# Attention with sinks with its value products turned round, gate steps and low parts of weights moved, and part of an expert search brought forward

## The chip, the core and the metric

One core of a Trainium2 chip runs the whole program. The metric is the device time of one execution in microseconds (us). The engines are PE (TensorE: matmuls and transposes), DVE (VectorE), ACT (ScalarE), POOL (GpSimd) and the DMA queues, which SP issues. Each engine works through its own list of instructions in order; semaphores hold an instruction until what it reads is written and what it overwrites is free.

## The reference

512 tokens of 1024 channels go through four stages in float32: (a) a gated delta-rule mixer; (b) attention in a window of 128 keys with a learned sink per head; (m) a mixer of an mLSTM and a forgetting attention; (p) a product-key retrieval over 16384 single-neuron experts. The parts that the change touches:

```python
# stage b: 32 query heads of 64, 4 key/value heads, blocks of 128 queries and 256 keys
m = max(max(logits), sink); p = exp(logits - m)
probs = p / (sum(p) + exp(sink - m))
o = probs @ v                       # per head
out = (o * silu(z)) @ w_out
# stage p: 8 heads, two half queries each, 128 sub-keys per half
val, idx = top_k(scores, 16)        # per token, head and half
cand = val[:, :, 0, :, None] + val[:, :, 1, None, :]      # 256 candidates
top_s, pos = top_k(cand, 16); gate = softmax(top_s)
```

## The kernel before, in words

A projection of float32 accuracy is three matmuls (`mm3`, lines 315 to 317): every weight panel of 128 x 1024 and the normed tokens are split into a rounded high part (`whi`, `hThi`) and the rest (`wlo`, `hTlo`). The high part of a panel is written by ACT (line 233, or 230 with a gain), the low part by DVE or, where `lo_on_pool` is true, by POOL (line 235). A `Feed` loads panels through SP into `wraw` and splits them ahead of use; its list `srcs` sets the order of the loads.

Most of the program is handed to a scheduler of the framework, which fixes each engine's list when the program is built; the order in which the code issues steps is its input. `weave` interleaves lists of steps in proportion to their lengths.

*Stage b* (`stage_b`, `block_b`). For each of four groups `g` of 8 heads there are queries (`queries`, 96 matmuls of 512 columns), gates (`gates`, 96 of them, tokens in the rows of the result), the attention itself and the output projection (`outputs`). The attention of a group has 8 units `u`: 4 blocks `n` of 128 queries times 2 halves `b` of 4 heads. `logits` (line 920) writes scores to PSUM, DVE adds the bias and takes the limit (line 923), ACT takes the exponential (line 929); `values` transposes the probabilities to `PT` (line 940, copies at 942); `products` (line 951) takes each head's `PT` tile of 128 x 128 as the weights and streams 64 columns of `V`; `finish` divides by the sum on DVE (line 958) and multiplies with the gate on POOL (line 960); `turn` transposes the result (line 966) and splits it into `yh` and `yl`. The attention of group g is woven with gates(g), outputs(g - 1) and queries(g + 1).

*Stage m*. The feed has 36 panels, whose low parts are POOL's. Projections of keys and queries are 36 steps; the mLSTM's gates are 11 small steps (`gates_m`), of which one is issued at step 4 and the others are woven with the next projection.

*Stage p*. `route1` norms and transposes the four token tiles, then for 16 half heads `hp` projects, takes scores (line 1593) and the 16 best of 128 for each tile with `top16` on DVE (lines 1565 to 1569). `route2` has for each token tile t eight steps `head(h)`, each the sum of two lists of 16 (`cand`, line 1613) and a `top16` over 256, and then gates, rows and a finish; `build_g` (DVE lines 1677 and 1682, POOL 1680 and 1684, PE 1690) spreads the chosen experts into a table in DRAM. Between them runs `First.work`, the first projection of blocks of experts (384 columns). The eight heads of tile 1 are issued after `route1`, woven with six such blocks. After `build_g` a list written by hand streams all experts (the last third of the time).

Of the kernel before, what the change touches and what calls it, by code (L numbers as in the profile page):

```python
# [7 lines left out]
F32 = mybir.dt.float32  # L8
# [10 lines left out]
P = 128  # L19
# [718 lines left out]
def stage_b(k):  # L738
    tc, nc, a = k.tc, k.nc, k.a
    with pool(tc, name="sb1", bufs=1) as s1:  # L740
# [12 lines left out]
        srcs, at = kv + wb(0), {("q", 0): 4}  # L753
        for g in range(4):
            for n, l in (("z", wb(4 + g)), ("o", wo(g - 1) if g else []), ("q", wb(g + 1) if g < 3 else [])):
                at[n, g - (n == "o") + (n == "q")] = len(srcs)
                srcs = srcs + l
# [4 lines left out]
        def keys(s2, acc):  # L762
            def use(t, p):
                kv = s2.tile([P, 512], F32, tag="sz", name="kv", bufs=6)
# [43 lines left out]
        def gates(g, s2):  # L808
            d = gs[g]

            def use(t, p):

                z = s2.tile([P, 512], F32, tag="sz", name="sz", bufs=6)
                nc.scalar.activation(z, p, AF.Tanh, scale=0.5)
                nc.vector.scalar_tensor_tensor(z, z, 1.0, p, op0=ALU.add, op1=ALU.mult)
                d["z"].append(z)

            return tiles_steps(k, feed, at["z", g], tiles, hh, hl, use)
# [16 lines left out]
        with pool(tc, name="sb2", bufs=1) as s2:  # L835
            with pool(tc, name="pgb", bufs=2, space=PSUM) as k.pg:
# [21 lines left out]
                for _, f in qs:  # L858
                    f()
            with pool(tc, name="pb", bufs=2, space=PSUM) as k.pb:  # L860
                pt = lambda: k.pb.tile([P, 512], F32, tag="pt", name="pt")
                left = []
                for g in range(4):
                    L, V_, O_, F, T_ = block_b(k, s1, s2, g, gs[g], kT, V, sinkrow)

                    attend = [lambda L=L: L(0)] + left
                    for u in range(8):
# [3 lines left out]
                        if u % 2 == 0 and u:  # L871
                            attend.append(lambda T_=T_, u=u: T_(u // 2 - 1))
                            if u == 4:
                                cut = len(attend) + 1
# [3 lines left out]
                    left = [lambda T_=T_: T_(NT - 1)]  # L878
                    fill = gates(g, s2)
                    if g:  # L880
                        fill += outputs(g - 1, (0, 1), False) + outputs(g - 1, (2, 3), False)
                    if g < 3:
                        qs = queries(g + 1, s2, pt)
                        left.append(qs[-1][1])
# [9 lines left out]
def block_b(k, s1, s2, g, d, kT, V, sinkrow):  # L894
# [37 lines left out]
    def values(u):  # L932
# [3 lines left out]
        for q in range(nst):  # L936
            pt = k.pb.tile([P, 512], F32, tag="pt", name="pt")
            for i in range(4):
                h, st = divmod(4 * q + i, nst)
                nc.tensor.transpose(pt[:, i * P : (i + 1) * P], lg[:, h, st * P : (st + 1) * P], k.ident)  # L940
            eng = nc.vector.tensor_copy if q else nc.scalar.copy
            eng(PT[:, 4 * q : 4 * q + 4, :], v4(pt))

    def products(u):
# [4 lines left out]
        for h in range(4):  # L949
            for st in range(nst):  # L950
                nc.tensor.matmul(d["po"][:, (4 * b + h) * 64 : (4 * b + h + 1) * 64], PT[:, h * nst + st, :],  # L951
                                 V[:, s0 // P + st, g * 64 : (g + 1) * 64], start=(st == 0), stop=(st == nst - 1))

    def finish(n):
        den = d["den", n]
        nc.vector.reciprocal(den, den)
        obs[n] = o = s2.tile([P, 512], F32, tag="ob", name="ob", bufs=2)
        nc.vector.tensor_tensor(out=o.rearrange("p (h c) -> p h c", h=8), in0=d["po"].rearrange("p (h c) -> p h c", h=8),
                                in1=den.rearrange("p (h o) -> p h o", o=1).to_broadcast([P, 8, 64]), op=ALU.mult)
        nc.gpsimd.tensor_tensor(out=o, in0=o, in1=d["z"][n], op=ALU.mult)  # L960

    def turn(n):
        o, ts = obs.pop(n), slice(n * P, (n + 1) * P)
        pt = v4(k.pb.tile([P, 512], F32, tag="pt", name="pt"))
        for i in range(4):
# [768 lines left out]
```

## Time and profile before

| what | value |
|---|---|
| median of 3 runs | 2784.94 us (2783.59 to 2785.3) |
| the profiled execution | 2783.23 us, its span 2781.5 us |
| PE, PEld, DVE busy | 96%, 80%, 71% of the span |
| ACT, POOL busy | 41%, 29% of the span |
| granted clock of TensorE | 0.986 of full speed in the mean |
| DMA | 440.92 MB, 159 GB/s in the mean |

The profile is of one execution. Matmuls are pipelined, so that the duration of one (about 0.40 us for 512 columns) is longer than the distance to the start of the next (about 0.23 us); costs of PE are read from start to start. A float32 matmul or transpose that is not split has records of its own: a matmul of line 951 has two (448 records for 224 matmuls). Groups of the trace name tiles as out<-in. Stages in the span: a to 612 us, b to 1082, m to 1447, p from there, with `route1` to 1574, `route2` and `build_g` to 1900.

### The profile page before, as it was taken

Reading aid. Unit: us, or ns where it says so; the run is one execution under the profiler, and the core shown is the slowest. Engines: PE = TensorE matmul, PEld = TensorE weight load, DVE = VectorE, ACT = ScalarE, POOL = GpSimd, SP = SyncE. Lnnn points to the kernel's source line nnn. Section 1 sums busy time; section 2 is a strip of 40 time slices with the busy share of each in tenths; the row PEclk is TensorE's granted clock in tenths of the full one; section 3 lists DMA queues with packets and bytes.
Section 4 is the critical chain, followed back from the end, with each engine's and each line's share of the span. In section 5 each row is a group of like instructions: output and inputs, shape, how many; then the busy total and the mean of one; then the engine's idle time right before and its main releaser. Section 6 shows DMA issues by size and latency. Waiting matters only on the chain.

```text
span 2781.5 us, 39306 instructions
## 1 busy us (share of the span) xinstructions
PE 2678.8 (96%) x14291; PEld 2222.2 (80%) x14291; DVE 1968.2 (71%) x4299; ACT 1127.4 (41%) x2304; POOL 810.0 (29%) x593
## 2 busy tenths in 40 slices
PE   7999999989999999999989898999999999999999
PEld 5777777767777777677668788999888888888887
DVE  6666666666666654646656999986777777878887
ACT  5444444434444343334422256554333333333333
POOL 0100000000000013232213158774444444444441
PEclk9999999999999999999999999999999999999999
DMA  4111111122222222211122244558999999898996
GB/s 153 53 54 61 54 61 54 46 69 76 65 72 76 68 69 68 61 61 31 32 105 70 87 159 172 184 203 284 325 329 327 321 320 329 312 324 317 329 322 234
DMA packets 170462, 440.92 MB, mean 159 GB/s; under 512 B 13932, under 2 KB 79756, under 8 KB 168604
## 3 DMA queue, kind: packets, MB, share of 16 engines
q1 hardware_dynamic: 133404, 304.17, 33.1%
q0 software_dynamic: 36864, 134.23, 12.7%
q8 instruction: 113, 1.85, 0.3%
q14 instruction: 81, 0.66, 0.1%
HBM read 401.60 MB, written 36.75 MB: 158 GB/s over the span
## 4 chain that ended last, share of the span: by engine, by line
PE 72%; DVE 14%; ACT 5%; issue 5%; POOL 2%; DMA 2%; SPq 0%; ACTq 0%; DVEq 0%; POOLq 0%
PE pj L315 12%; PE pj L316 12%; PE pj L317 12%; PE acc L316 4%; PE acc L317 4%; PE acc L315 4%; PE pG L1690 2%; PE po L951 2%; ACT whio L233 2%; DVE x L1558 1%; DVE wloo L235 1%; PE pl L920 1%; PE po L316 1%; PE po L315 1%; PE po L317 1%
## 5 line engine op out<-in xcount | busy, mean ns | idle before, releaser
L315 PE MATMUL pj<-hThi,whi 128*128 128x384 f32 (+2 forms) x1664 | 604.1, 363 | 2.7 <-ACT hg L1436 2.1
L317 PE MATMUL pj<-hThi,wlo 128*128 128x384 f32 (+2 forms) x1664 | 594.5, 357 | 11.9 <-DVE wlo L235 11.9
L316 PE MATMUL pj<-hTlo,whi 128*128 128x384 f32 (+2 forms) x1664 | 598.6, 360 | 0.0
L317 PEld LDWEIGHTS pj<-hThi,wlo 128*128 128x128 f32 x1664 | 317.8, 191 | 33.8 <-DVE wlo L235 12.5
L315 PEld LDWEIGHTS pj<-hThi,whi 128*128 128x128 f32 x1664 | 317.9, 191 | 32.6 <-ACT hg L1436 2.7
L316 PEld LDWEIGHTS pj<-hTlo,whi 128*128 128x128 f32 x1664 | 318.2, 191 | 25.0 <-issue 1.3
L316 PE MATMUL acc<-wloo,Wh 128*128 128x512 f32 x768 | 302.9, 394 | 4.0 <-DVE wloo L235 2.4
L315 PE MATMUL acc<-whio,Wh 128*128 128x512 f32 x768 | 300.8, 392 | 0.8 <-ACT whio L233 0.8
L317 PE MATMUL acc<-whio,Wl 128*128 128x512 f32 x768 | 300.3, 391 | 0.0
L1549 POOL DMA_INDIRECT raw<-in_v_dram,ids x128 | 192.1, 1501 | 236.1 <-DVE wloo L235 122.8
L1549 POOL DMA_INDIRECT raw<-in_u_dram,ids x128 | 185.8, 1452 | 241.4 <-DVE wloo L235 114.9
L212 ACT CAST Wh<-W 128x384 fp32r<-128x384 f32 x128 | 65.7, 513 | 372.5 <-DVE W L1496 335.7
L235 DVE TENSOR_TENSOR wlo<-raw,whi 128x1024 fp32r<-128x1024 f32 x128 | 161.5, 1262 | 71.9 <-ACT whi L233 71.8
L233 ACT CAST whi<-raw 128x1024 fp32r<-128x1024 f32 x144 | 150.3, 1043 | 123.3 <-issue 90.1
L235 DVE TENSOR_TENSOR wloo<-raw,whio 128x1024 fp32r<-128x1024 f32 x128 | 156.9, 1226 | 52.2 <-ACT whio L233 52.2
L316 PEld LDWEIGHTS acc<-wloo,Wh 128*128 128x128 f32 x768 | 144.2, 188 | 44.4 <-DVE wloo L235 16.8
L317 PEld LDWEIGHTS acc<-whio,Wl 128*128 128x128 f32 x768 | 144.2, 188 | 30.4
L315 PEld LDWEIGHTS acc<-whio,Wh 128*128 128x128 f32 x768 | 144.1, 188 | 29.5 <-ACT whio L233 1.6
L1558 DVE SCALAR_TENSOR_TENSOR x<-raw,act,x 128x1024 f32<-128x1024 f32 x128 | 163.8, 1280 | 1.0
L1553 DVE SCALAR_TENSOR_TENSOR raw<-raw,xt 128x1024 f32<-128x1024 f32 x128 | 154.0, 1219 | 0.0
L233 ACT CAST whi<-wraw 128x1024 fp32r<-128x1024 f32 x100 | 104.6, 1048 | 113.7 <-PE pj L316 70.0
L1436 ACT ACTIVATE hg<-pj 128x384 f32<-128x384 f32 x128 | 62.6, 489 | 190.1 <-PE pj L317 190.1
(423 smaller groups left out, 5417.8 us busy)
## 6 DMA issues: line engine op xcount, KB each, us to landing
raw<-in_uT_dram SPq DMA_DIRECT2D x128, 512.0 KB
raw<-in_v_dram SPq DMA_DIRECT2D x128, 512.0 KB
wraw<-in_wa_dram SPq DMA_DIRECT2D x48, 512.0 KB
G<-stage SPq DMA_DIRECT2D x12, 2048.0 KB
Gt<-G SPq DMA_DIRECT2D x32, 768.0 KB
wraw<-in_wb_dram SPq DMA_DIRECT2D x32, 512.0 KB
wraw<-in_wmt_dram SPq DMA_DIRECT2D x20, 512.0 KB
H<-hg SPq DMA_DIRECT2D x48, 192.0 KB
```

Source lines behind the costliest of these rows:

```text
L212: self.nc.scalar.copy(hi, src)
L233: nc.scalar.copy(hi, raw)
L235: eng.tensor_tensor(out=lo, in0=raw, in1=hi.bitcast(F32), op=ALU.subtract)
L315: nc.tensor.matmul(out, wh, mh, start=first, stop=False)
L316: nc.tensor.matmul(out, wh, ml, start=False, stop=False)
L317: nc.tensor.matmul(out, wl, mh, start=False, stop=last)
L951: nc.tensor.matmul(d["po"][:, (4 * b + h) * 64 : (4 * b + h + 1) * 64], PT[:, h * nst + st, :], V[:, s0 // P + st, g * 64 : (g + 1) * 64], ...
L1436: nc.scalar.activation(hg, p[:, 0:ND], AF.Gelu)
L1549: nc.gpsimd.indirect_dma_start(out=g, out_offset=None, in_=src, in_offset=bass.IndirectOffsetOnAxis(ap=ids[:, j : j + 1], axis=0))
L1553: nc.vector.scalar_tensor_tensor(g, g, 1.0, xt0, op0=ALU.mult, op1=ALU.mult, accum_out=act[:, j : j + 1])
L1558: nc.vector.scalar_tensor_tensor(k.x[:, 0, :], g, act[:, j : j + 1], k.x[:, 0, :], op0=ALU.mult, op1=ALU.add)
L1690: nc.tensor.matmul(p[:, n * P : (n + 1) * P], o1[:, n, :], o0[:, n, :], start=True, stop=True)
```

## The change

In stage b the probabilities are streamed and `V` is the weight: a matmul takes 64 columns of `V` and streams two heads (256 columns), and the two heads of a pair (`j`) write to the two halves of the array's columns. The result has channels in its rows, so it needs no transposing; the gates are projected with channels in rows too, and the reciprocal sums are spread by ACT over 64 columns per head, transposed by PE and multiplied into the gate (`sums`). The gates of group g are computed one group earlier, those of group 0 ahead of the attention. In stage m the low parts go from POOL to DVE and the gate steps are issued at every fourth step from step 5. In stage p the norm of a tile is issued one tile ahead, the low parts of the first two panels go to DVE, and head(h) of tile 1 is issued after half head 2h + 1 of `route1`. The rest of the diff only passes pools and tiles along.

```diff
-        srcs, at = kv + wb(0), {("q", 0): 4}
+        srcs, at = kv + wb(0) + wb(4), {("q", 0): 4, ("z", 0): 8}
         for g in range(4):
-            for n, l in (("z", wb(4 + g)), ("o", wo(g - 1) if g else []), ("q", wb(g + 1) if g < 3 else [])):
+            for n, h, l in (("o", g - 1, wo(g - 1) if g else []), ("q", g + 1, wb(g + 1) if g < 3 else []), ("z", g + 1, wb(5 + g) if g < 3 else [])):
...
+            def step(j, c):
+                if j == c == 0:
+                    d["z"] = s2.tile([P, 4, T], F32, tag="sz", name="sz", bufs=2)
+                if c == 0:
+                    d["p"] = k.acc()
+                p, (wh, wl) = d["p"], feed.get(at["z", g] + c, 1)[0]
+                for i in range(2):
+                    kt, ws = 2 * c + i, slice(512 * i + P * j, 512 * i + P * j + P)
+                    mm3(nc, p, wh[:, ws], wl[:, ws], hh[:, kt, 0:T], hl[:, kt, 0:T], kt == 0, kt == KD - 1)
...
-                for _, f in qs:
+                for _, f in qs + gates(0, s2):
...
-                        if u % 2 == 0 and u:
-                            attend.append(lambda T_=T_, u=u: T_(u // 2 - 1))
+                        if u % 2:
+                            attend.append(lambda S=S, u=u: S(u // 2))
...
-                    fill = gates(g, s2)
+                    fill = []
                     if g:
                         fill += outputs(g - 1, (0, 1), False) + outputs(g - 1, (2, 3), False)
...
-                        weave(attend, fill + qs[:-1])
+                        weave(attend, fill + qs[:-1] + gates(g + 1, s2))
                         continue
                     o = outputs(3, range(4), True)
-                    weave(attend[:cut], fill)
-                    weave(attend[cut:] + left, o[:4])
+                    weave(attend, fill + o[:4])
...
+        if b:
+            den = d["den", n]
+            nc.vector.reciprocal(den, den)
+            obs[n] = ob = s2.tile([P, 4, P], F32, tag="ob", name="ob", bufs=2)
+            nc.scalar.copy(ob.rearrange("p i (j c) -> p (i j) c", j=2), den.rearrange("p (h o) -> p h o", o=1).to_broadcast([P, 8, 64]))
+
+    def sums(n):
...
+            nc.tensor.transpose(pt[:, i * P : (i + 1) * P], ob[:, i, :], k.ident)
+        nc.vector.tensor_tensor(out=z, in0=v4(pt), in1=z, op=ALU.mult)
...
-        for h in range(4):
-            for st in range(nst):
-                nc.tensor.matmul(d["po"][:, (4 * b + h) * 64 : (4 * b + h + 1) * 64], PT[:, h * nst + st, :],
-                                 V[:, s0 // P + st, g * 64 : (g + 1) * 64], start=(st == 0), stop=(st == nst - 1))
+        for st in range(nst):
+            for j in range(2):
+                nc.tensor.matmul(d["po"][64 * j : 64 * j + 64, 2 * b * P : 2 * (b + 1) * P], V[:, s0 // P + st, g * 64 : (g + 1) * 64],
+                                 PT[:, 4 * st + 2 * j : 4 * st + 2 * j + 2, :].rearrange("p i c -> p (i c)"), start=(st == 0), stop=(st == nst - 1))
...
     def finish(n):
...
-        nc.gpsimd.tensor_tensor(out=o, in0=o, in1=d["z"][n], op=ALU.mult)
...
+        nc.vector.tensor_tensor(out=o, in0=v4(d["po"]), in1=d["z"][:, :, ts], op=ALU.mult)
+        k.split(d["yh"][:, :, ts], d["yl"][:, :, ts], o)
...
-                + [(a["wmt"][4 + c], None) for c in range(4)] + [(a["wmo"][4 * c + 2 * h + j], None) for h in range(2) for c in range(2) for j in range(2)], 6)
+                + [(a["wmt"][4 + c], None) for c in range(4)] + [(a["wmo"][4 * c + 2 * h + j], None) for h in range(2) for c in range(2) for j in range(2)], 6, lo_on_pool=False)
...
-                        if n == 4:
+                        if n % 4 == 1 and n > 4:
                             gates.pop(0)()
...
-                route1(k, raw, s0, s2, hh, hl, xt0, val, idx)
+                route1(k, raw, s0, s2, hh, hl, xt0, val, idx, route[1][0][0:8])
...
-                weave(route[1][0], early(n))
+                weave(route[1][0][8:], early(n))
...
     for t in range(NT):
-        xn = k.normed(s0, t, k.rms(s0, t), g)
-        if t == 0:
-            nc.gpsimd.tensor_copy(xt0, xn)
+        nx = norm(t + 1) if t + 1 < NT else None
         k.turn(xn, hh, hl, t * P)
+        xn = nx
...
-        pan = k.halves(r, lo_on_pool=True, bufs=2)
+        pan = k.halves(r, lo_on_pool=hp > 1, bufs=2)
...
+        if hp % 2:
+            heads[hp // 2]()
```

What moves is seen best in the engines' lists. PE in stage b, around one unit's value products (`po` is their result, `pj` that of a projection). Before:

```order
L315 MATMUL pj<-whi,yh 128x512
L316 MATMUL pj<-wlo,yh 128x512
L317 MATMUL pj<-whi,yl 128x512
L951 MATMUL po<-V,PT 128x64 x8
L315 MATMUL pj<-whi,yh 128x512
```

After the change:

```order
L962 MATMUL pt<-cst,ob 128x128 x4
L315 MATMUL pj<-whi,hThi 128x512
L316 MATMUL pj<-wlo,hThi 128x512
L317 MATMUL pj<-whi,hTlo 128x512
L315 MATMUL pj<-whi,hThi 128x512
L316 MATMUL pj<-wlo,hThi 128x512
L317 MATMUL pj<-whi,hTlo 128x512
L973 MATMUL po<-PT,V 64x256 x4
L315 MATMUL pj<-whi,hThi 128x512
```

Eight matmuls of 64 columns have become four of 256 columns on half of the array's columns. Of 24 units with two key tiles 20 have their four in one piece, three have two and two, one has one and three; the 8 units with one key tile have two.

DVE in stage m, where the forgetting attention begins (`fqn` is a normed query tile, `colR` and `colC` gate columns, `dB` a tile of decay). Before:

```order
L310 TENSOR_TENSOR fqn<-pq,rr 128x512
L1219 COPY colR<-pt 16x96
L1220 COPY colC<-pt 16x8
L1219 COPY colR<-pt 128x96
L1220 COPY colC<-pt 128x8
...
L1347 TENSOR_SCALAR dB<-ncB,colC 128x144 x2
L1347 TENSOR_SCALAR dB<-ncB,colC 128x272
L1360 ISA dB,fmm<-pl,dB 128x144
```

After the change:

```order
L310 TENSOR_TENSOR fqn<-pq,rr 128x512
L235 TENSOR_TENSOR wlo<-wraw,whi 128x1024
L1233 COPY colR<-pt 128x96
L1234 COPY colC<-pt 128x8
...
L235 TENSOR_TENSOR wlo<-wraw,whi 128x1024 x2
L1361 TENSOR_SCALAR dB<-ncB,colC 128x144
L235 TENSOR_TENSOR wlo<-wraw,whi 128x1024
L1361 TENSOR_SCALAR dB<-ncB,colC 128x144
L1361 TENSOR_SCALAR dB<-ncB,colC 128x272
L235 TENSOR_TENSOR wlo<-wraw,whi 128x1024
```

Low parts that stood in POOL's list now stand between DVE's steps of the attention.

DVE at the end of `route1` (`psc` are scores, `cand` and `top` belong to a head). Before, the list goes on after the last scores with eight heads:

```order
L235 TENSOR_TENSOR wlo<-raw,whi 128x1024
L1568 MAX val<-scr 128x8
L1569 MAX_INDEX idx<-val,scr 128x8
L1613 TENSOR_TENSOR cand<-val 128x256 x2
L1565 MAX top<-cand 128x8 x2
L1566 MAX_INDEX pos<-top,cand 128x8
```

After the change only the eighth head is left there, and rows follow:

```order
L1636 TENSOR_TENSOR cand<-val 128x256
L1586 MAX val<-scr 128x8
L1583 MAX top<-cand 128x8
L1587 MAX_INDEX idx<-val,scr 128x8
...
L1661 CAST xf<-idx 128x128
L1586 MAX top<-scr_13943 128x8
L235 TENSOR_TENSOR wlo<-raw,whi 128x1024
L1587 MAX_INDEX pos<-top,scr_13943 128x8
L1644 TENSOR_TENSOR pe<-top 128x128
```

Seven heads have moved up between the `top16` of `route1`, and the third block's low part now comes behind one head, not behind seven.

## Rows read from the trace of the kernel before

**Rows 1.** Busy time by stretch: window, PE, PEld, DVE, ACT, POOL, clock, DMA.

```profile
690.00:1060.00 370.00, 363.77 (x2015) 289.51 (x2015) 226.98 (x664) 162.81 (x439) 25.40 (x18) 1.00 0.22 68
...
1082.00:1200.00 118.00, 110.14 (x514) 84.57 (x513) 57.35 (x147) 39.15 (x55) 31.52 (x16) 0.97 0.21 65
1200.00:1447.00 247.00, 240.17 (x1386) 175.61 (x1385) 141.57 (x431) 93.99 (x235) 60.60 (x51) 0.97 0.14 42
1447.00:1470.00 23.00, 13.91 (x61) 11.02 (x60) 11.22 (x21) 7.79 (x13) 6.48 (x3) 0.78 0.58 226
1470.00:1574.00 104.00, 104.00 (x517) 85.84 (x516) 85.06 (x516) 25.83 (x33) 31.46 (x14) 1.00 0.27 82
1574.00:1840.00 266.00, 235.31 (x1482) 230.00 (x1481) 260.03 (x548) 147.04 (x313) 172.44 (x114) 0.95 0.47 165
```

**Rows 2.** Waits of PE, 685 to 1082 us: total, times, longest.

```profile
PE pt L797 <- DVE qn L310: 3.7, 6, 0.9
```

**Rows 3.** Waits of PE, 1080 to 1440 us.

```profile
PE pt L1034 <- DVE rr L188: 5.4, 1, 5.4
PE ptz L1108 <- DVE so L1059: 3.4, 1, 3.4
PE pc L278 <- ACT ncB L1331: 1.5, 1, 1.5
```

**Rows 4.** Waits of PE, 1440 to 1900 us.

```profile
PE pj L317 <- DVE wlo L235: 11.9, 2, 8.9
...
PE pt L264 <- DVE xn L254: 7.8, 1, 7.8
```

**Rows 5.** Timeline of PE in stage b: start, time, instructions merged.

```profile
708.14 1.89 PE L951 MATMUL po<-V,PT 128*128 128x64 f32 x16
709.84 0.48 PE L315 MATMUL pj<-whi,hThi 128*128 128x512 f32 x1
...
711.41 1.14 PE L920 MATMUL pl<-kT,qT 64*128 64x256 f32 x8
712.48 0.50 PE L315 MATMUL pj<-whi,hThi 128*128 128x512 f32 x1
```

**Rows 6.** Timeline of PE in stage m, value products of the forgetting attention.

```profile
1254.09 0.28 PE L316 MATMUL pj<-hTlo,whi 128*128 128x264 f32 x1
1254.20 0.28 PE L317 MATMUL pj<-hThi,wlo 128*128 128x264 f32 x1
1254.42 1.23 PE L1378 MATMUL fo<-fPT,FV 16*64 16x128 f32 x14
1255.58 0.91 PE L1288 MATMUL pS<-mqk,mqk 128*128 128x384 f32 x2
```

**Rows 7.** Groups by line and shape, 690 to 1060 us: DVE's low parts, ACT's copies.

```profile
L235 DVE TENSOR_TENSOR wlo<-wraw,whi 128x1024 fp32r<-128x1024 f32 x16 | 20.5, 1286 | 5.6 <-ACT whi L233 5.6
L942 ACT COPY PT<-pt 128x512 f32<-128x512 f32 x32 | 18.5, 579 | 20.3 <-PE pt L940 20.2
```

**Rows 8.** Groups by line and shape, POOL, 1075 to 1440 us.

```profile
L235 POOL TENSOR_TENSOR wlo<-wraw,whi 128x1024 fp32r<-128x1024 f32 x33 | 80.9, 2461 | 131.5 <-ACT whi L233 129.5 <-DVE dB L1347 2.0
```

**Rows 9.** Timeline of DVE in stage m, during two low parts of POOL.

```profile
1137.52 2.21 DVE L198 SCALAR_TENSOR_TENSOR rr<-rt,rr 128x8 f32<-128x8 f32 x1
1139.65 0.16 DVE L186 TENSOR_SCALAR rt<-rv 128x8 uint32<-128x8 uint32 x1
1139.72 2.84 DVE L213 TENSOR_TENSOR grow<-gu,grow 4x528 fp32r<-4x528 f32 x1
```

**Rows 10.** Busy time by stretch, just after that wait (columns as in rows 1).

```profile
1143.30:1149.20 5.90, 5.89 (x16) 4.75 (x17) 5.16 (x14) 2.86 (x4) 1.33 (x1) 0.50 0.24 83
```

**Rows 11.** Waits of DVE, 1470 to 1574 us.

```profile
DVE val L1565 <- PE psc L1593: 26.3, 16, 8.9
```

**Rows 12.** Timeline of DVE after route1: two heads' first instructions.

```profile
1584.25 0.41 DVE L1613 TENSOR_TENSOR cand<-val 128x256 f32<-128x256 f32 x1
...
1586.42 0.41 DVE L1613 TENSOR_TENSOR cand<-val 128x256 f32<-128x256 f32 x1
```

More of the change, by code (lines that the diff above doesn't have):

```diff
@@ L809, in gates @@
             d = gs[g]
[L811 to L818, printed above, removed]
+            def step(j, c):
[7 more added lines that the diff above has]
+                    mm3(nc, p, wh[:, ws], wl[:, ws], hh[:, kt, 0:T], hl[:, kt, 0:T], kt == 0, kt == KD - 1)
+                if j == 3:
+                    feed.done = at["z", g] + c + 1
+                if c == 3:
+                    z = d["z"][:, j, :]
+                    nc.scalar.activation(z, p, AF.Tanh, scale=0.5)
+                    nc.vector.scalar_tensor_tensor(z, z, 1.0, p, op0=ALU.add, op1=ALU.mult)
+                feed.step()
+            return [(1.3, lambda j=j, c=c: step(j, c)) for j in range(4) for c in range(4)]
         def outputs(g, js, last):
@@ L948, in products @@
             d["po"] = k.pb.tile([P, 512], F32, tag="pv", name="po", bufs=1)
-        for h in range(4):
-            for st in range(nst):
-                nc.tensor.matmul(d["po"][:, (4 * b + h) * 64 : (4 * b + h + 1) * 64], PT[:, h * nst + st, :],
-                                 V[:, s0 // P + st, g * 64 : (g + 1) * 64], start=(st == 0), stop=(st == nst - 1))
+        for st in range(nst):
+            for j in range(2):
+                nc.tensor.matmul(d["po"][64 * j : 64 * j + 64, 2 * b * P : 2 * (b + 1) * P], V[:, s0 // P + st, g * 64 : (g + 1) * 64],
+                                 PT[:, 4 * st + 2 * j : 4 * st + 2 * j + 2, :].rearrange("p i c -> p (i c)"), start=(st == 0), stop=(st == nst - 1))
     def finish(n):
[L955 to L959, printed above, removed]
-        nc.gpsimd.tensor_tensor(out=o, in0=o, in1=d["z"][n], op=ALU.mult)
[L962 to L965, printed above, removed]
-            nc.tensor.transpose(pt[:, i, :], o[:, i * P : (i + 1) * P], k.ident)
-        k.split(d["yh"][:, :, ts], d["yl"][:, :, ts], pt)
-    return logits, values, products, finish, turn
+        ts = slice(n * P, (n + 1) * P)
+        o = s2.tile([P, 4, P], F32, tag="ob", name="ob", bufs=2)
+        nc.vector.tensor_tensor(out=o, in0=v4(d["po"]), in1=d["z"][:, :, ts], op=ALU.mult)
+        k.split(d["yh"][:, :, ts], d["yl"][:, :, ts], o)
+    return logits, values, products, sums, finish
 def stage_m(k):
@@ L1458, in stage_p @@
         early = lambda n: [f.all for f in take(firsts, n)]
-        with pool(tc, name="pg", bufs=4, space=PSUM) as k.pg, pool(tc, name="spT", bufs=1) as sT:
+        with pool(tc, name="pg", bufs=4, space=PSUM) as k.pg, pool(tc, name="spT", bufs=1) as sT, ExitStack() as es:
             val = sT.tile([P, NT, 16, 16], F32, name="val")
             idx = sT.tile([P, NT, 16, 16], U32, name="idx")
+            sh = es.enter_context(pool(tc, name="sph", bufs=2))
+            where = {}
+            route = [route2(k, sh, where, t, val, idx, ids, gate0) for t in range(NT)]
             with pool(tc, name="spr", bufs=1) as s0, pool(tc, name="spr2", bufs=2) as s2:
-                route1(k, raw, s0, s2, hh, hl, xt0, val, idx)
+                route1(k, raw, s0, s2, hh, hl, xt0, val, idx, route[1][0][0:8])
             with pool(tc, name="sps", bufs=1) as s0, pool(tc, name="sps2", bufs=2) as s2:
@@ L1466, in stage_p @@
                 nc.vector.tensor_copy(iota16, k.c["iota"][:, 0:16])
-                route = [route2(k, s0, s2, t, val, idx, ids, gate0, iota16) for t in range(NT)]
+                where.update(s0=s0, s2=s2, iota16=iota16)
                 n = SPILL // 8
-                weave(route[1][0], early(n))
+                weave(route[1][0][8:], early(n))
                 for t in range(1, NT):
@@ L1569, in top16, with route1 @@
     nc.vector.max_index(out=idx[:, 8:16], in_max=val[:, 8:16], in_values=scr)
-def route1(k, raw, s0, s2, hh, hl, xt0, val, idx):
+def route1(k, raw, s0, s2, hh, hl, xt0, val, idx, heads):
     tc, nc, a = k.tc, k.nc, k.a
@@ L1654, in finish @@
             nc.tensor.transpose(pt[:, i * P : (i + 1) * P], s, k.ident)
-        res["selT"] = s2.tile([P, 3, P], F32, tag="selT", name="selT")
+        res["selT"] = where["s2"].tile([P, 3, P], F32, tag="selT", name="selT")
         nc.scalar.copy(res["selT"], pt[:, 0 : 3 * P].rearrange("p (i c) -> p i c", i=3))
```

43 lines of the change are left out of this document (23 added, 20 removed).

## The prediction

> **What bounds the kernel now.** I read the busy times by stretch first [rows 1]. The reader is to see three kinds of stretch. In stage b, 690 to 1060 us, PE is busy 364 of 370 us at full clock, DVE 227, ACT 163: PE sets the time, and what is taken from PE there shortens the program. In stage m, 1082 to 1447, PE is busy 350 of 365, DVE only 199, and the clock is 0.97: PE again, with a few stops. In stage p the two parts differ: in `route1`, 1470 to 1574, PE is busy all the time and DVE 85 of 104; from 1574 to 1840 DVE is busy 260 of 266 and PE 235, so there DVE sets the time. At 1447 to 1470 neither is full: a chain. Then I read what PE waits for in each. In b the largest is 3.7 us in six pieces [rows 2], so next to nothing; in m three waits of 5.4, 3.4 and 1.5 us [rows 3]; in p 11.9 us for low parts of panels on DVE, of which one wait is 8.9 us, and 7.8 us for a normed tile [rows 4].
>
> **The change, part by part.** The sum is made against the profiled execution, 2783.2 us; the median of the runs, 2784.9, lies 1.7 above it.
>
> *1. Value products.* A unit with two key tiles is 16 records of 64 columns from 708.14 to the next start at 709.84, 1.70 us [rows 5]; the 8 units with one key tile have half of that, 0.85. Before: 24 x 1.70 + 8 x 0.85 = 47.6 us, all of it on PE. After, such a unit is 8 records of 256 columns on two halves of the array's columns. Two rows are near. The scores are 8 records of 256 columns too, on two halves of the array's rows, and take 711.41 to 712.48, 1.07 us [rows 5]. The value products of the forgetting attention have just the new arrangement, halves of the columns: 16 records of 128 columns (two are missing in the row), which is the same number of columns, take 1254.42 to 1255.58, 1.16 us, and the matmul ahead of them needs 0.22 us to their start where its neighbour needs 0.11 [rows 6]. I take the second, as it is the same arrangement: 1.16 + 0.10 = 1.26 us for eight records. For a piece of four I take no gain, 0.85. By the order of the changed list there are 20 pieces of eight, 14 of four, and one unit in pieces of two and six (1.7 at most): 25.2 + 11.9 + 1.7 = 38.8 us. Gain 47.6 - 38.8, **-9 us**. Bounds: at 1.07 for eight and 0.64 for four, without anything at the ends, 21.4 + 9.0 + 1.3 = 31.7, a gain of 16; if the halves don't overlap, eight records of 256 columns cost the five steps of 1.07 made eight, 1.7, and the entry of 0.1 for 36 pieces makes it 4 slower.
>
> The Trainium skill (TensorEngine Tiling (Array Packing), Key Properties) says that changing the tiling mode drains the array. It speaks against many short pieces, and the 0.22 us of rows 6 agrees; without it the gain would be the 16, with it the 9.
>
> *2. The rest of stage b.* The 64 transposes of the result are replaced by 64 of the spread sums, equal. The gates have the same 96 matmuls per group; those of group 0 now stand without attention beside them, and the attention of group 3 has 22 us less beside it. I cost that at nothing: PE is the full engine wherever they stand. ACT gets 16 copies of 0.58 us [rows 7], DVE 16 multiplications of 512 values, about 0.64 by half of the 1.29 for 1024 [rows 7], and POOL loses 16. This is hidden under PE; without that cover it would be 20 us. SP issues the same 52 loads with queries ahead of gates; PE waits for no panel in rows 2.
>
> *3. Low parts in stage m.* 36 panels leave POOL, where one takes 2.46 us [rows 8], and cost DVE 36 x 1.29 = 46 us [rows 7]. DVE has 365 - 199 = 166 us free there [rows 1], so it does not fill. What leaves is a stop: while POOL writes low parts, a DVE instruction on 8 values takes 2.21 us and one on 528 values 2.84, where a third on 8 values between them takes 0.16 [rows 9]. These two stand in the chain to the 5.4 us wait of PE [rows 3], and behind it PE runs 5.9 us at a clock of 0.50 [rows 10], that is 1.2 GHz after an idle stretch, which loses another 2.9. The gate steps, which fill DVE there too, are spread out. Of these 8.3 us I take 7 as gone, since low parts of 1.29 us now stand in the same chain. The wait of 3.4 us [rows 3] has a POOL low part beside it as well, but a DVE low part now stands just ahead of the awaited instruction: I take 2. Of the 1.5 us, which ACT ends, 1. Together **-10 us**. Bounds: -15 if all these go with their slow clock; +5 if each of the 36 passes on a tenth of itself and nothing goes.
>
> *4. Start of stage p.* PE waits 7.8 us for the last normed tile [rows 4]. The code issues it earlier, but it needs the last sum of stage m in any case, and the list of DVE has it where it was. Two low parts, 2 x 1.29, enter that chain and a stop like that of rows 9 leaves it: **-1 us**, bounds 0 and -5.
>
> *5. Heads.* Two heads start 1584.25 and 1586.42, 2.17 us apart [rows 12]; eight are 17.4 us of DVE. They leave the stretch where DVE is full [rows 1] and enter `route1`, where DVE waits 26.3 us in 16 pieces for scores, 8.9 of them at the start, so 17.4 in use [rows 11]. That just fits: at 6.5 us per half head, two of them leave 2 x 1.2 us for one head of 2.17. The last head needs the last scores and stays behind: 17.4 - 2.2 = 15.2 us gained on DVE. PE's 8.9 us wait for a low part behind these heads [rows 4] is part of it and not counted again. What is late next is PE itself: it has 31 us idle in that stretch, so it can follow. **-15 us**, bounds -4 and -20 (the wait with its slow clock).
>
> Sum: -9 - 10 - 1 - 15 = -35; 2783.2 - 35 = 2748.2, and 1.7 above it for the median: **2750 us**.
>
> **Rivals.**
>
> *Halves do not overlap in part 1* for 256 columns: 2750 + 9 = 2759. Against it stands the forgetting attention [rows 6], with 128. Chance 0.10.
>
> *The heads do not fit into* `route1`. Their first instruction adds two lists in SBUF, and POOL still writes the low parts of 14 panels of 2.46 us there; if it starts inside one, it stands for about 2 us as in rows 9, 8 times 2 = 16 us, and DVE comes out of `route1` as late as before: about 2764. For it: the fit is exact [rows 11, 12]. Against it: the head starts as the list puts it, about 0.3 us ahead of POOL's next start in my count. Chance 0.13.
>
> The Trainium skill (SBUF — State Buffer, Who interferes with whom) says that a VectorE instruction with two SBUF inputs contends with a GpSimd one that reads SBUF, and the later one blocks for all of it. Rows 9 agree, and it would give this rival wherever the starts fall so.
>
> *More goes:* in m all three waits and in p 20 us: 2750 - 5 - 5, and 7 from part 1 without anything at the ends, some 2733. Chance 0.12.
>
> *Slower: DVE's list in stage m becomes PE's bound.* Each low part stands in front of a step that PE needs at once, and PE waits it out: +46 us in place of -10, with -25 from the other parts: 2784.9 + 21 = 2806. It decides when more than 25 of the 46 us reach PE's waits. Against it: PE waits only some 10 us there now [rows 3] and DVE is busy about half. Chance 0.04.
>
> *Nothing of it counts*, the stages being held by something that the waits don't name: 2785. Chance 0.03.
>
> **How the numbers follow.** The forecast has 0.58. The range should hold 8 in 10: 2728 to 2772 takes in the first three rivals and most of the bounds, and leaves out the last two and the ends of several parts at once. A measurement of this kernel can tell about 0.2%, 5.6 us, from no change: faster 0.58 + 0.10 + 0.13 + 0.12 = 0.93, same 0.03, slower 0.04.
>
> **What would show it.** Part 1 is right if a unit's eight records take 1.1 to 1.3 us to the next start; at 1.7 the halves don't overlap. Part 3 is right if the 5.4 us wait and the slow clock after it are gone and PE's waits on DVE in m do not grow. Part 5 is right if DVE has almost no idle time in `route1`, PE's 8.9 us wait is gone, and the table's first products come some 15 us earlier after the last scores; with heads' first instructions of 2 us the second rival holds. The forecast is wrong if stage b is not some 9 us shorter from 612 on, or if the stretch after 1574 is as long as before.

## The result and the profile after

The change took the kernel from 2785.12 us (4 runs, 2783.59 to 2786.05) to **2742.2 us** (4 runs, 2741.34 to 2743.41): a ratio of 0.9844, 95% interval 0.9829 to 0.9860. Forecast were 2750 us, between 2728 and 2772. The profiled execution took 2743.41, 39.8 less than the one before. The busy times on its page:

```profile
PE 2658.4 (97%) x14067; PEld 2178.1 (79%) x14067; DVE 1981.1 (72%) x4353; ACT 1135.3 (41%) x2320; POOL 680.1 (25%) x539
```

PE lost 20 us of work and POOL 130; DVE gained 13. To see where the time went I take, in both traces, lines that open or close a stretch. The view of one source line gives its engine, number, durations in ns, and the first and last start in us. Before: L776 turns keys at the start of stage b, L1012 is stage m's first product, L1034 transposes its normed queries, L1378 makes the value products of the forgetting attention, L1593 the scores of `route1`, L1690 the table.

```profile
L776 PE MATMUL pv<-kv,cst x8: 379/380/382, 636.3 to 661.9; 128*128 128x256 f32 x8
L1012 PE MATMUL pm<-cst,mj x8: 207/208/231, 1069.3 to 1069.8; 16*128 16x16 f32 x8
L1034 PE MATMUL pt<-cst,fqn x36: 208/273/444, 1119.9 to 1176.5; 128*128 128x128 f32 x32, 16*128 16x16 f32 x4
L1378 PE MATMUL fo<-fPT,FV x224: 267/273/393, 1217.1 to 1413.8; 128*64 128x128 f32 x80, 16*64 16x128 f32 x32
L1593 PE MATMUL psc<-kyT,pqT x128: 275/275/377, 1468.7 to 1567.7; 128*128 128x128 f32 x128
L1690 PE MATMUL pG<-o,o x768: 270/275/579, 1614.6 to 1900.2; 128*128 128x128 f32 x192
```

The same lines after the change:

```profile
L776 PE MATMUL pv<-kv,cst x8: 379/380/382, 638.7 to 664.1; 128*128 128x256 f32 x8
L1025 PE MATMUL pm<-cst,mj x8: 207/208/230, 1053.8 to 1054.2; 16*128 16x16 f32 x8
L1047 PE MATMUL pt<-cst,fqn x36: 207/272/327, 1104.4 to 1156.2; 128*128 128x128 f32 x32, 16*128 16x16 f32 x4
L1392 PE MATMUL fo<-fPT,FV x224: 267/273/469, 1190.3 to 1387.4; 128*64 128x128 f32 x80, 16*64 16x128 f32 x32
L1614 PE MATMUL psc<-kyT,pqT x128: 275/275/377, 1441.0 to 1539.9; 128*128 128x128 f32 x128
L1714 PE MATMUL pG<-o,o x768: 270/275/579, 1570.3 to 1860.8; 128*128 128x128 f32 x192
```

| stretch | from, to | before | after | change | forecast |
|---|---|---|---|---|---|
| b | last of L776, first of L1012 (L1025) | 407.4 | 389.7 | -17.7 | -9 |
| m | first of L1034 (L1047), last of L1378 (L1392) | 293.9 | 283.0 | -10.9 | -10 |
| chain | from there to the first score | 54.9 | 53.6 | -1.3 | -1 |
| loop | first score, last score | 99.0 | 98.9 | -0.1 | 0 |
| table | last score, last product of the table | 332.5 | 320.9 | -11.6 | -15 |

These make -41.6; 2.2 us came in ahead of b and 0.4 left the rest. The whole, 39.8, is 4.8 us more than the forecast 35. Two terms are off in opposite directions, b by 9 and the table by 3, and so cancel in part: that the whole is so near is partly luck.

*Stage b.* PE's timeline after the change, a piece of four records and one of eight:

```profile
754.19 0.65 PE L973 MATMUL po<-PT,V 128*64 128x256 f32 x4 [0.33 <-DVE PT L950]
754.77 0.50 PE L315 MATMUL pj<-hThi,whi 128*128 128x512 f32 x1
...
762.81 0.39 PE L317 MATMUL pj<-hThi,wlo 128*128 128x512 f32 x1
763.12 1.08 PE L973 MATMUL po<-PT,V 128*64 128x256 f32 x8
764.14 0.50 PE L315 MATMUL pj<-hThi,whi 128*128 128x512 f32 x1
```

Eight records take 1.02 us to the next start, where 16 took 1.70 [rows 5]; four take 0.58. At the entry the matmul ahead needs 0.31 us to their start instead of 0.23: 0.08 for the change of shape. That makes 20 x 1.10 + 14 x 0.66 + 1.7 = 33 us in place of 47.6, which is 14.6 less. Summed from start to next start over the whole stage, the records of `po` take 47.7 us before and 31.3 after, and with some 3 us for 36 entries the gain is about 13.5. The rest of b's 17.7 comes from work that the change didn't touch, the scores: their records (`pl`) sum to 40.8 us before and 35.9 after, 4.9 less, and all other work grew by less than 1. Their groups by shape, before and after, hold the same 192 instructions:

```profile
L920 PE MATMUL pl<-kT,qT 64*128 64x256 f32 x192 | 33.5, 404 | 0.0
```

```profile
L928 PE MATMUL pl<-kT,qT 64*128 64x256 f32 x192 | 29.4, 404 | 0.0
```

The mean of one is equal, the busy time 4.1 us less: more of them ran side by side. PE's timeline before shows why. A unit of eight [rows 5] is four records on each half of the array's rows; where the scheduler cut a unit in two, a piece could hold one half alone:

```profile
803.01 1.13 PE L920 MATMUL pl<-kT,qT 64*128 64x256 f32 x4
804.06 0.51 PE L315 MATMUL pj<-whi,yh 128*128 128x512 f32 x1
...
813.88 0.70 PE L920 MATMUL pl<-kT,qT 64*128 64x256 f32 x2
814.51 0.50 PE L315 MATMUL pj<-whi,yh 128*128 128x512 f32 x1
```

Four records of one half alone take 1.05 us, as long as eight on both (1.07): `logits` issues the two matmuls of one half first, then those of the other. Of the units with two key tiles the list of before has three cut in 2 + 2 matmuls and four in 1 + 3, that of after three in 1 + 3 and none in 2 + 2.

*Stage m.* The three largest waits of PE from 1080 to 1420 after the change:

```profile
PE fo L1392 <- ACT fPT L1384: 2.2, 3, 1.6
PE pt L1047 <- DVE fqn L310: 1.4, 2, 0.8
PE pt L1047 <- DVE rv L206: 1.2, 1, 1.2
```

The waits of 5.4, 3.4 and 1.5 us [rows 3] are gone. But nearly all the gain lies ahead of the forgetting attention: from the first L1034 to the first L1378 it took 97.2 us, now 85.9, which is -11.3; from there to the last it took 196.7 and takes 197.1. In that second part PE's waits fell from 5.1 us to 2.8 only, since the one for ACT grew from 0.6 to 2.2. The slow clock behind the wait of 3.4 (0.50 from 1388.2 to 1391.6) went with it, but another stretch at half clock came (the seventh figure is the clock), in which PE is busy all the time:

```profile
1268.00:1271.00 3.00, 3.00 (x13) 2.35 (x12) 2.02 (x7) 0.58 (x2) 0.00 (x0) 0.51 0.00 0
```

So 2.3 us less of waiting left the part no shorter; what made PE's work there 2.7 us longer is open.

*`route1` and the table.* DVE waits for scores 14.8 us, 8.7 of them at the start, in place of 26.3 [rows 11]; the loop has its length. The largest waits of PE from 1540 to 1880 are:

```profile
PE pG L1714 <- POOL o L1708: 7.4, 6, 4.8
PE pj L317 <- DVE wlo L235: 4.6, 4, 1.6
PE pG L1714 <- POOL o L1704: 3.9, 5, 1.3
```

The wait of 8.9 us for a low part [rows 4] is gone, the longest is 1.6. The waits for POOL are not new. Before, from 1440 to 1900, they were 16.2 us:

```profile
PE pG L1690 <- POOL o L1684: 10.5, 5, 5.5
PE pG L1690 <- POOL o L1680: 5.7, 6, 1.6
```

The first product of the table comes 46.9 - 30.4 = 16.5 us earlier after the last score, but the last only 11.6. The busy times from the last score to the first product, before and after (PE's is the first after the length, with its number of instructions), show why:

```profile
1567.70:1614.60 46.90, 32.83 (x162) 31.07 (x160) 44.41 (x146) 13.81 (x19) 1.60 (x2) 0.82 0.30 94
```

```profile
1539.90:1570.30 30.40, 26.79 (x142) 25.49 (x141) 29.05 (x85) 13.06 (x19) 2.18 (x2) 0.94 0.40 123
```

Twenty matmuls of the blocks now stand behind the first product and no longer ahead of it. At 0.19 us each (26.79 / 142) they are an estimated 3.8 us of the 16.5, which come back before the last product.

### The profile page after: what moved, and what is told of

Its sections match the earlier page's. It is cut to its first block, busy times and chain, and to the rows that moved or that the text cites. A ratio compares the mean times of both kernels' runs of the same rounds, so it can differ in the third digit from the quotient of the medians.

```text
span 2741.6 us, 38815 instructions
## 1 busy us (share of the span) xinstructions
PE 2658.4 (97%) x14067; PEld 2178.1 (79%) x14067; DVE 1981.1 (72%) x4353; ACT 1135.3 (41%) x2320; POOL 680.1 (25%) x539
## 4 chain that ended last, share of the span: by engine, by line
PE 72%; DVE 16%; ACT 5%; issue 4%; DMA 2%; POOL 1%; ACTq 0%; SPq 0%; DVEq 0%; POOLq 0%
PE pj L315 12%; PE pj L316 12%; PE pj L317 12%; PE acc L316 5%; PE acc L317 4%; PE acc L315 4%; PE pG L1714 2%; ACT whio L233 2%; DVE wlo L235 1%; DVE wloo L235 1%; PE pq L317 1%; DVE x L1576 1%; PE pq L315 1%; PE pq L316 1%; PE po L316 1%
## 5 line engine op out<-in xcount | busy, mean ns | idle before, releaser
L315 PE MATMUL pj<-hThi,whi 128*128 128x384 f32 (+2 forms) x1792 | 656.5, 367 | 2.0 <-ACT hg L1450 1.9
L316 PE MATMUL pj<-hTlo,whi 128*128 128x384 f32 (+2 forms) x1792 | 648.1, 362 | 0.2 <-DVE hTlo L213 0.2
L317 PE MATMUL pj<-hThi,wlo 128*128 128x384 f32 (+2 forms) x1792 | 643.8, 359 | 4.6 <-DVE wlo L235 4.6
L315 PEld LDWEIGHTS pj<-hThi,whi 128*128 128x128 f32 x1792 | 340.7, 190 | 42.6 <-issue 7.6
L317 PEld LDWEIGHTS pj<-hThi,wlo 128*128 128x128 f32 x1792 | 340.5, 190 | 33.1 <-DVE wlo L235 5.9
L316 PEld LDWEIGHTS pj<-hTlo,whi 128*128 128x128 f32 x1792 | 340.9, 190 | 29.7 <-issue 1.2
L316 PEld LDWEIGHTS acc<-wloo,Wh 128*128 128x128 f32 x768 | 144.2, 188 | 44.0 <-DVE wloo L235 16.2
L235 DVE TENSOR_TENSOR wlo<-wraw,whi 128x1024 fp32r<-128x1024 f32 x100 | 123.0, 1231 | 54.0 <-ACT whi L233 53.0
```

The costliest lines, as they stand in the source:

```text
L235: eng.tensor_tensor(out=lo, in0=raw, in1=hi.bitcast(F32), op=ALU.subtract)
L315: nc.tensor.matmul(out, wh, mh, start=first, stop=False)
L316: nc.tensor.matmul(out, wh, ml, start=False, stop=False)
L317: nc.tensor.matmul(out, wl, mh, start=False, stop=last)
```

## The experiments

All start from the changed kernel unless said otherwise. The stretches in each run's profiled execution are read as above. The kernel before was measured again beside each: it took 2788.5 us beside halves apart, low parts on POOL, gate steps and three heads more, and 2785.5 or 2785.6 beside the others. So times of different rows are compared by their ratios:

| run | b | m | chain | loop | table | median of runs, us | ratio to before |
|---|---|---|---|---|---|---|---|
| the change | 389.7 | 283.0 | 53.6 | 98.9 | 320.9 | 2742.2 | 0.9844 (0.9829 to 0.9860) |
| the change again | 389.3 | 288.2 | 52.8 | 98.7 | 323.7 | 2746.5 | 0.9862 (0.9845 to 0.9878) |
| halves apart | 391.8 | 283.0 | 53.9 | 98.9 | 325.2 | 2749.0 | 0.9859 (0.9833 to 0.9884) |
| b back | 408.0 | 286.3 | 52.8 | 98.8 | 320.0 | 2768.2 | 0.9943 (0.9926 to 0.9960) |
| low parts of m on POOL | 393.7 | 296.8 | 53.1 | 98.9 | 323.5 | 2758.8 | 0.9890 (0.9872 to 0.9908) |
| gate steps as before | 388.9 | 288.3 | 52.9 | 98.9 | 330.2 | 2749.3 | 0.9856 (0.9838 to 0.9873) |
| heads issued behind | 389.5 | 285.6 | 54.3 | 98.9 | 319.2 | 2736.5 | 0.9824 (0.9807 to 0.9840) |
| the same again | 389.5 | 282.9 | 53.6 | 98.9 | 318.8 | 2741.1 | 0.9835 (0.9816 to 0.9853) |
| heads barred | 388.9 | 282.6 | 53.7 | 98.9 | 335.4 | 2756.2 | 0.9892 (0.9870 to 0.9914) |
| three heads more | 389.0 | 286.0 | 53.9 | 98.9 | 331.8 | 2750.7 | 0.9859 (0.9841 to 0.9878) |
| table to ACT | 389.3 | 283.0 | 53.9 | 98.9 | 317.2 | 2739.4 | 0.9834 (0.9817 to 0.9850) |
| both | 389.7 | 287.4 | 53.0 | 98.9 | 309.9 | **2734.7** | **0.9809 (0.9792 to 0.9827)** |

**The change again.** No edit.

> The changed kernel once more, as the measure for the others beside it, since the kernel before took 2788.5 us in the last runs and 2785.1 in the first. Theory A, all times of this place are some 0.1% higher: 2745 to 2746, every stretch ahead of the table within 1 us of the first profile. Theory B, the table's stretch (from the first product of the table to its last) differs from run to run by itself, by POOL's and DVE's timing against each other: 290.6 us long in the first profile, here anything from 285 to 302, and the time follows it.

A's time came, but not its stretches: with nothing changed stage m was 5.2 us longer and the table 2.8, of which the part from its first product to its last took 293.2, as B allows. The six profiles whose stage p is that of the changed kernel have tables of 320.0 to 330.2. So stage m of one profile is known to some 5 us and the table to some 10, and smaller effects are read from rows. Where the five of stage m come from stands in the last section.

**Halves apart.**

```diff
-        for st in range(nst):
-            for j in range(2):
+        for j in range(2):
+            for st in range(nst):
```

> The changed kernel (2742.2 us) with the value products of a unit issued first for one half of the array's columns, over both key tiles, and then for the other; the same matmuls in another order. Theory A, two matmuls on different halves run side by side only when they stand next to each other: a unit of eight records takes about 1.6 us to the next start instead of 1.01 (the middle two of the four matmuls still pair up: three steps of 0.43 and what lies at the ends), 24 units give 10 to 15 us, and the kernel takes 2752 to 2757. Theory B, the gain of the turned products comes from fewer records or fewer weights to load: 1.0 us as before, 2742.

PE's timeline of a unit there:

```profile
761.68 1.09 PE L973 MATMUL po<-PT,V 128*64 128x256 f32 x8
762.70 0.50 PE L315 MATMUL pj<-hThi,whi 128*128 128x512 f32 x1
```

1.02 us as before the edit; b is 2.1 us longer. The list cuts its units at other places (four of them into two and six records, where the changed kernel has one so), some pieces take up to 1.76 us, and the records of `po` sum to 34.2 us against 31.3. Theory A fell: two matmuls of one half, then two of the other, run side by side all the same. B's number for the unit came; its 2742 did not, but the ratio, 0.9859, lies between the changed kernel's two. B's reason doesn't follow: four records on one half alone cost 1.05 us in the scores, so the eight in 1.02 do share the time. The Trainium skill (TensorEngine Tiling (Array Packing), Key Properties) says that tiles, the parts into which the array is divided, operate independently; this run agrees, with its 1.02 us.

**Stage b back.** `stage_b` and `block_b` as in the kernel before.

> The changed kernel with stage b as before (values streamed, result transposed, gates with tokens in rows beside their group's attention), all else as changed; expected as a difference from the changed kernel beside it. Theory A, stage b's gain is its own: its length goes back from 390 to 407 us (the last step of the keys to the first transpose of stage m), 17 slower, with the scores taking 41 us of PE and not 36, the value products 48 and not 31. Theory B, part of it belongs to the work around it: 9 to 13 slower.

Its b is 408.0, 18.3 more than after: theory A. The gain of b is its own, and the scores' part of it goes and comes with that stage's order: summed from start to start their records take 40.9 us here, and the value products 47.7, as before the change. The median is 21.7 above the changed kernel beside it; the profiled execution is the fastest of the four, and where the others lost 6 to 11 us more isn't known. The stage was put back as a whole, so no run tests its gates and sums by themselves.

**Low parts of m on POOL.**

```diff
-...], 6, lo_on_pool=False)
+...], 6)
```

> The changed kernel (2742.2 us) with the low parts of stage m's 36 panels back on POOL, the gate steps where the change put them. Theory A, POOL's low parts hold up small DVE instructions in the chains that PE waits for: a wait of PE for the normed query tiles of 3 to 6 us comes back with a stretch at half clock behind it, the kernel takes 2748 to 2752. Theory B, the gain in stage m came from spreading the gate steps: 2741 to 2744. Theory C, the low parts on DVE cost something by themselves: 2738 to 2741.

The largest waits of PE from 1080 to 1420 there:

```profile
PE pt L1047 <- DVE rv L206: 5.0, 1, 5.0
PE pt L1047 <- DVE fqn L310: 3.6, 2, 3.0
PE ptz L1122 <- DVE so L1073: 3.2, 1, 3.2
```

And DVE's timeline, two instructions of the norm and the gate steps, here and in the changed kernel:

```profile
1123.36 1.83 DVE L198 SCALAR_TENSOR_TENSOR rr<-rt,rr 128x8 f32<-128x8 f32 x1
1125.22 2.80 DVE L1218 TENSOR_TENSOR gR<-gl,gE 4x528 f32<-4x528 f32 x1
```

```profile
1120.59 0.14 DVE L198 SCALAR_TENSOR_TENSOR rr<-rt,rr 128x8 f32<-128x8 f32 x1
...
1120.77 0.70 DVE L1218 TENSOR_TENSOR gR<-gl,gE 4x528 f32<-4x528 f32 x1
```

1.83 us against 0.14, 2.80 against 0.70, while two low parts run on POOL from 1122.80 to 1127.47: the stops are POOL's. Theory A's waits came. Stage m takes 296.8, which is 13.8 more than in the changed kernel's first profile and 8.6 more than in its second; before the change it took 293.9. So spreading the gate steps alone gives nothing that shows above the spread. The time grew by more than theory A said. b grew by 4 too: POOL's first two low parts of stage m run there from 1018.9 to 1024.1, and PE then waits 2.3 us for the spread sums `ob` and 0.9 for `yl`, which it doesn't in the changed kernel.

**Gate steps as before.**

```diff
-                        if n % 4 == 1 and n > 4:
+                        if n == 4:
```

> The changed kernel (2742.2 us) with the gate steps of stage m placed as before (one at step 4, ten woven with the third projection), the low parts on DVE. Theory A (POOL's low parts were the cause): within 3 us of it, 2741 to 2745, PE's waits in stage m before the attention below 3 us. Theory B (crowded gate steps were the cause): the 5 us wait of PE is back, 2748 to 2752.

Stage m took 288.3, as in the second profile of the changed kernel (288.2), and the waits that end on the norm are 1.6 us in two pieces and 1.3. By the waits it is theory A: where the gate steps stand hardly matters once POOL is out of the way. The time, 2749.3, lies in B's range, but its ratio, 0.9856, is between the changed kernel's two. The profiled execution was the slowest of the four (2754.9), and most of what it has more is its table (330.2), which this edit does not touch.

**Heads issued behind the loop.**

```diff
-        if hp % 2:
-            heads[hp // 2]()
...
-                weave(route[1][0][8:], early(n))
+                weave(route[1][0], early(n))
```

> The changed kernel with all eight heads of tile 1 behind the loop over half heads again, as before; expected as a difference from the changed kernel beside it. Theory A, what reaches the end is PE's idle time and slow clock that the heads caused (from the last scores to the last product of the table 332.5 us before and 320.9 after): 11.6 us slower. Theory B, all DVE time taken away counts: 15.2 us slower. Theory C, the heads inside the loop cost as much as they save: within 2 us. In A and B PE's wait of about 9 us for a low part behind the heads is back.

None of the three: 2736.5 us, 10 less than the changed kernel beside it. In DVE's list seven of the eight heads still stand between the `top16` of the loop. They had not moved back: the code's order is an input of the scheduler, and I took it that it raises them wherever their memory is free, which the run with the heads barred tests. What the line does change comes behind the loop: without it the twenty matmuls stand ahead of the table's first product again, as before the change. The four times lay between 2735.9 and 2746.1, so I ran it again:

> The kernel with the heads issued behind the loop again, the same program as the run that took 2736 us three times and 2746 once. Theory A, one program has two courses of the table's stretch about 10 us apart, chosen anew in each execution: times of both kinds, around 2736 and around 2746. Theory B, the one of 2746 was an exception: all within 2 us of 2736.

2738.6 to 2744.9, spread over the range: neither theory, no two distinct courses. In both runs the kernel is no slower without the line.

**Heads barred.** The heads' own pool (`sph`) is opened only after the loop, so that their tiles lie where the loop's were, as in the kernel before; the heads are issued there.

> The changed kernel with the heads' pool opened only behind the loop over half heads, and the heads issued there; in the run before, where only the issue was put back, the heads still stood in the loop, since the scheduler raised them into memory of their own. Now their tiles lie where the loop's tiles were, as in the kernel before, and the eight heads follow the loop. Theory A, what reaches the end is PE's idle time and slow clock behind those heads: 8 to 13 us slower than the changed kernel (2742 to 2746), so 2751 to 2758, with PE's wait of about 9 us for a low part back. Theory B, the gain at this place came from something else (the order of the blocks' low parts): within 4 us of the changed kernel.

2756.2, table 335.4, 14.5 longer than after the change, and 16.4 longer than the mean of the two runs before, from which this one differs only in where the pool is opened. The two largest waits of PE from 1540 to 1880:

```profile
PE pG L1712 <- POOL o L1706: 13.0, 9, 5.5
PE pj L317 <- DVE wlo L235: 9.9, 2, 7.5
```

Theory A. So the gain at the table belongs to the heads' move, and what moves them is the pool, not the line in the loop.

**Three heads more.**

```diff
+        if hp in (5, 9, 13):
+            more[(hp - 5) // 4]()
...
+                del route[2][0][0:3]
```

> The changed kernel (2742.2 us) with three heads of tile 2 as well inside the loop over half heads (behind half heads 5, 9 and 13), taken out of the work beside the table. Theory A, DVE sets the time from the last scores to about 1800 us, and what leaves it there shortens the program by three quarters of it, as it did for the seven heads: 3 x 2.17 x 0.76 = 5 us less, 2737; DVE still fits into the loop, which leaves it 0.99 us in 13. Theory B, PE, full from 1800 us to the end of the table, sets the end: 2742 within 1. Theory C, the loop becomes DVE's: the last scores' successors come 2 us or more later and the time is 2743 to 2746.

Not faster, so A fell. That it is slower, as C says, isn't shown: the ratio, 0.9859, lies between the changed kernel's two, and the loop keeps its 98.9 us. After it PE waits:

```profile
PE pj L317 <- DVE wlo L235: 11.9, 2, 10.3
```

The changed kernel starts this block's low part at 1539.55, between the `top16` of the last scores. Here the list of DVE puts it behind all of them, at 1547.84, and PE stands 10.3 us for it, where the kernel before had 8.9. Another thing shows in the loop. Three of its ten `cand` take 1.23 to 1.64 us, the others 0.41, and each of the three starts inside a low part of POOL. The first of them, beside a low part that runs from 1477.76 to 1480.14:

```profile
1479.19 1.23 DVE L1639 TENSOR_TENSOR cand<-val 128x256 f32<-128x256 f32 x1
```

**Table to ACT.**

```diff
-        if b % 4 in (1, 3):
+        if b % 4 == 1:
             nc.gpsimd.tensor_tensor(out=o0, in0=o0, in1=col(2), op=ALU.mult)
```

> The changed kernel with 24 of the table's 48 multiplications of 512 values taken from POOL and given to ACT (four of 128 values, 0.32 us each, 31 us on ACT, which is busy 130 of 214 us there); expected as a difference from the changed kernel beside it. Theory A, PE's waits for POOL in the table (11.3 us in the first profile) are part of what sets the time, and fewer POOL instructions make them smaller: 4 to 8 us faster. Theory B, DVE, full there, sets the time alone: within 2 us. Theory C, ACT comes late with the blocks' high parts: 3 us slower or more.

7.0 us less than the changed kernel beside it, with the table at 317.2: A's number. Its reason isn't borne out, since PE's waits for POOL there are 12.3 us, where the changed kernel has 11.3 in its first profile and 12.7 in its second. The intervals overlap too, so that the gain itself is likely and not shown.

**Both**, heads issued behind and the table's multiplications on ACT.

> The changed kernel with the heads issued behind the loop (the scheduler raises them by itself) and 24 of the table's 48 multiplications on ACT. Theory A, both save PE's waits in the table's stretch, and not the same ones: 2730 to 2736. Theory B, they remove the same waits: 2736 to 2740. Theory C, the gain of either was chance of timing between POOL and DVE: 2740 to 2746.

2734.7 us (five runs, 2732.69 to 2736.32), the fastest version, and its interval lies below that of the changed kernel in both of its measurements. The table takes 309.9, and PE's largest waits there are:

```profile
PE pG L1712 <- POOL o L1702: 7.1, 7, 1.8
PE pG L1712 <- POOL o L1706: 3.7, 2, 2.9
PE pj L317 <- DVE wlo L235: 3.3, 3, 1.5
```

A's number came, and the table is 7 to 9 us shorter than with either edit alone, though the intervals of the times overlap with theirs. Again it is not POOL: the waits for it are 10.8 us, with the heads issued behind alone they were 8.3 and 8.5. What fell are the waits for low parts, from 7.2 to 3.3; why is open.

## Why the prediction held, point by point

*Value products, -9 forecast, -13.5 to -14.6 measured.* The mechanism was right and the size of a term was off: "1.26 us for eight records", taken from the forgetting attention [rows 6], measured 1.10 with its entry, and a piece of four, for which I took no gain, 0.66 instead of 0.85. The scores, which I had set aside as the other arrangement, were the better row: 1.07 there, 1.02 here. The rival that halves don't overlap is out; of the 7 us that "more goes" adds here, some 5 came.

*"I cost that at nothing", the rest of b.* It gave 3 to 4 us. The step that failed is to take the untouched matmuls as equal: their pieces changed with the scheduler's list. The rows for it were there before (a piece of four of one half at 803 us), and I had not asked what a cut unit costs.

*Stage m, -10 forecast, -10.9 measured.* POOL's low parts were the stop, as the run with them on POOL shows. But the three terms were not 7, 2 and 1. Ahead of the attention, where 7 and 1 stood, it gave 11.3: with the wait of 1.5 went a slow clock behind it (0.50 from 1208 to 1214 us before), which I had not counted. In the attention the wait of 3.4 went, but the term of 2 gave nothing.

*Start of stage p, -1 forecast, -1.3 measured.* As the prediction said, the awaited norm stays: PE waits 6.7 us in place of 7.8. No run puts this part back alone.

*Heads, -15 forecast, -11.6 measured, -8.8 in the second profile.* They fit: all seven `cand` in the loop take 0.41 or 0.42 us, so the rival with POOL in its way did not come. It was close: the first `cand` starts at 1452.80 and POOL's next low part at 1453.27, and with three heads more three of them were caught. The step that failed is "PE can follow". From the last score to the last product DVE's work fell by 16.6 us, from 307.6 to 291.0, as the sum wanted, but the stretch by 11.6, and in the six profiles of this stage p by 2 to 13. PE still waits 21.8 us there (30.2 before), 11.3 of them for POOL's parts of the table; the sum took it that DVE's 15 us reach the table's end in full, past these waits. Of the 16.5 us by which the first product came earlier, the sign I had named, some 4 are only order. And the sentence that the rest of the diff only passes pools along missed the cause of the move: it is the pool that lets the heads rise.

The slower rival is out: with the low parts of m on DVE no wait of PE on DVE there is above 1.2 us.

## What to carry to other kernels

Where a scheduler orders the lists, ask of each move what allowed it: here memory of its own let the heads rise, and the line that was to move them was not needed. Price a packed matmul by the fuller of the two halves, and look for pieces that the scheduler cut so that one half runs alone (four records in 1.05 us, eight on both halves in 1.07). When a stretch starts earlier, count what stands ahead of its first instruction before and after: some of the gain may be order. And read a stretch in more than one execution of the same program before a few microseconds of it are given a cause.

## What the runs showed that I had not expected

*POOL starved over many instructions.* The same two multiplications of the table in two executions of the same program; POOL's timeline after the change and in its second profile:

```profile
1631.22 1.41 POOL L1708 TENSOR_TENSOR o<-o,selT 128x512 f32<-128x512 f32 x1 [0.53 <-DVE o L1701]
1638.16 5.50 POOL L1708 TENSOR_TENSOR o<-o,selT 128x512 f32<-128x512 f32 x1 [5.52 <-DVE o L1701]
```

```profile
1630.84 10.20 POOL L1708 TENSOR_TENSOR o<-o,selT 128x512 f32<-128x512 f32 x2 [1.36 <-DVE o L1701]
```

The shortest such multiplication takes 1.03 us. In the second execution DVE runs without a gap until 1639.1, and then itself waits for POOL; PE waits 8.4 us for the result:

```profile
1642.28 0.80 DVE L1701 TENSOR_TENSOR o<-cst,selT 128x512 f32<-128x512 f32 x1 [3.14 <-POOL o L1704]
```

The Trainium skill (SBUF — State Buffer, Who interferes with whom) says that the one that comes second blocks for the whole of the other's instruction. Here it is held up over a row of them. That this makes the table's spread of 320.0 to 330.2 us, in runs that leave stage p alone, is read from such rows and was not tested by itself.

*The clock fell in one execution and not in the other.* In the second profile of the changed kernel PE waits 2.24 us for ACT from 1354.7, and from 1358 its clock is 0.57 in the mean; in the first the same wait is 1.6 and the clock stays up. Busy times of that place in the program, which comes 4 us later in the first; second profile, then first:

```profile
1358.00:1370.00 12.00, 11.90 (x36) 7.59 (x37) 4.67 (x11) 3.49 (x7) 0.00 (x0) 0.57 0.22 77
```

```profile
1362.00:1374.00 12.00, 11.90 (x55) 7.75 (x56) 8.58 (x18) 3.69 (x9) 0.46 (x1) 1.00 0.29 85
```

In equal busy time PE had 36 matmuls in the one and 55 in the other. That and the longer wait are the 5 us by which stage m differs between the two. The length of the wait doesn't tell it alone: with the gate steps as before the longest was 1.5 us, and the clock was 0.50 from 1361 to 1370 too. What decides it is open.
